# Attention's TensorE instructions in written order, values two steps behind their scores, queries prepared in thirds

## The chip, the cores and the metric

One core of one Trainium2 chip runs the whole program, a two-layer network, in one launch. The metric is the device time of an execution in microseconds (us); lower is better. The engines are TensorE (PE in the profile; PEld is its weight loads), VectorE (DVE), ScalarE (ACT), GpSimd (POOL) and the queue of SyncE (SP), which issues the loads.

## The reference, cut to what matters

Layer 0 is attention over 256 latent and 256 context tokens with 16 heads of 64 and 4 key/value heads. Each latent query sees rotated keys of its window and unrotated context keys; a context query sees context keys alone; a sink logit joins each softmax.

```python
s_win = jnp.einsum('blgrd,bsgd->bgrls', qb, kw) * scale      # rotated q, k; masked to the window
s_ctx = jnp.einsum('blgrd,bsgd->bgrls', qpb, k_c) * scale    # plain q, context k
p = sink_softmax(jnp.concatenate([s_win, s_ctx], axis=-1))
o = einsum(p[..., :SPAN], vw) + einsum(p[..., SPAN:], v_c)
y_lat = o.reshape(...) @ w_out                               # then layer norm, MLP, layer 1 (SSM), MLP
```

## The kernel before

All is float32. A large product is split in a high and a low part (`wh`, `wl`; `u0h`, `u0l`), three matmuls for each tile of 128 (`gemm`, lines 79 to 81). Attention runs over eight pairs of heads, p = 0 to 7, and in each over three items t: t = 0 and 1 are the two blocks of latent queries, t = 2 is both blocks of context queries. Item (p, t) is

- `scores`: ten matmuls (eight for t = 2) into two PSUM banks `s`; DVE takes the maxima (`TENSOR_REDUCE`, lines 461 and 467) and three small operations; ACT does the exponentials into `P` (line 477); DVE two small operations and the division (line 484);
- `mix`: eight transposes `pt` of `P` on PE (line 497), two ACT copies to `PT`, eight (t = 2: four) value matmuls `o` (line 503; each is two rows of the profile), an ACT copy and a DVE subtraction into `oh`, `ol`.

`q_gemm(p)` makes the queries of a pair: 24 matmuls `q` of 512 columns, copied by ACT to `qf`; `q_parts(p)` splits and rotates them on ACT and DVE into `qe, qo, re, ro`, which the scores of pair p read. `filler` is a generator of 27 steps on the modulation vectors: 24 groups of four matmuls `mod<-wm` (line 93), each on its own 512 KB load `wm` with two buffers, and three outputs of two transposes each. The PSUM tags are `mm` (4 banks: scores, most of the query products), `aux` (3: transposes, values) and `md` (1).

Nothing fixes PE's order: every engine executes its own list in order, and a scheduler makes the lists when the program is built, by its own estimate of what is ready. In the code an item's `mix` follows the next item's `scores`; the lists that come out cut one operation's matmuls into another's. Whatever follows attention (the output projection `ao`, and loads that need attention's buffers) starts as attention ends.

Of the kernel before, what the change touches and what calls it, by code (L numbers as in the profile page):

```python
# [8 lines left out]
F32 = mybir.dt.float32  # L9
F32R = mybir.dt.float32r  # L10
# [29 lines left out]
class Net:  # L40
# [23 lines left out]
    def next_w(self, ahead=2, whole=False):  # L64
# [7 lines left out]
            return wh, wl  # L72
        return wh.rearrange("p (k c) -> p k c", c=128), wl.rearrange("p (k c) -> p k c", c=128)

    def gemm(self, ps, w, ah, al, c0, c1, ks=range(8)):
        mm = self.nc.tensor.matmul
        wh, wl = w
        for k in ks:
            mm(ps, wh[:, k, :], ah[k][:, c0:c1], start=(k == 0), stop=False)  # L79
            mm(ps, wh[:, k, :], al[k][:, c0:c1], start=False, stop=False)  # L80
            mm(ps, wl[:, k, :], ah[k][:, c0:c1], start=False, stop=(k == 7))  # L81
# [8 lines left out]
    def mods_mm(self, ps, k, wm):  # L90
        n = wm.shape[1] // 4
        for j in range(4):
            self.nc.tensor.matmul(ps[32 * j:32 * j + 32, 0:n], self.cs[:, k, :], wm[:, j * n:(j + 1) * n],
                                  start=(k == 0), stop=(k == 7))

    def mods_out(self, i, ps, n, cuts, streams=(0, 1)):

        nc = self.nc
        m4 = self.tmp.tile([128, 256], F32, tag="t1", name="m4")[:, :n]
        nc.scalar.copy(m4, ps[:, 0:n])  # L100
        q = n // 128
        pt = ps[:, 256:512]
        for c in range(q):
            nc.tensor.transpose(pt[:, c * 128:(c + 1) * 128], m4[:, c * 128:(c + 1) * 128], self.ident)
        ptv = pt[:, :n].rearrange("p (c j r) -> p j c r", c=q, j=4)
        for j0, w, t in cuts:
            bm = self.vec("bmod")[:, i * 48 + t:i * 48 + t + w]
            for v in streams:
                nc.vector.tensor_tensor(self.mT[i][:, v, t:t + w].rearrange("p (j c) -> p j c", c=q),
                                        ptv[:, j0:j0 + w // q, :, v], bm.rearrange("p (j c) -> p j c", c=q),  # L110
                                        op=ALU.add)
            if 8 <= t < 16 or t == 32:
                m = self.mT[i][:, streams[0]:streams[-1] + 1, t:t + w]
                nc.vector.tensor_scalar(m, m, 1.0, None, op0=ALU.add)
# [44 lines left out]
        yield  # L159

    def run(self, gen):
        for _ in gen:
            pass


    def affine(self, name, gv, bv, streams, scale, shift):
# [271 lines left out]

    def scores(self, p, t, q):
        nc = self.nc  # L440
        mm = nc.tensor.matmul
        qe, qo, re, ro = q
        g = p // 2
        P = [self.ap.tile([128, 512], F32, tag="P", name=f"P{p}{t}{a}", bufs=4) for a in range(2)]
        T = 1 if t < 2 else 2
        mx = self.ap.tile([128, 2, 8], F32, tag="st", name=f"st{p}{t}")
        bs = []
        for a in range(2):
            ps = self.bank("mm", f"s{p}{t}{a}")
            bs.append(ps)  # L450
            plain, rot = (qe, re) if a == 0 else (qo, ro)
            if t < 2:
# [4 lines left out]
                   start=False, stop=True)  # L457
# [24 lines left out]
        for a in range(2):  # L482
            for tt in range(T):
                nc.vector.tensor_scalar(P[a][:, tt * w:tt * w + w], P[a][:, tt * w:tt * w + w],
                                        sm[:, a, tt:tt + 1], None, op0=ALU.mult)
        return P

    def mix(self, p, t, P):
        nc = self.nc
        g = p // 2  # L490
        PT = [self.ap.tile([128, 512], F32, tag="PT", name=f"PT{p}{t}{a}", bufs=3) for a in range(2)]
        for a in range(2):
            pt = self.bank("aux", f"pt{p}{t}{a}")
            for c in range(4):

                o = c if t < 2 else 2 * (c % 2) + c // 2
                nc.tensor.transpose(pt[:, o * 128:o * 128 + 128], P[a][:, c * 128:c * 128 + 128], self.ident)
            nc.scalar.copy(PT[a], pt)
        n, keys = (128, range(4)) if t < 2 else (256, range(2, 4))
        po = self.bank("aux", f"o{p}{t}")[:, :n]  # L500
        for i, kt in enumerate(keys):
            for a in range(2):
                nc.tensor.matmul(po[64 * a:64 * a + 64, :], self.V[:, kt, g * 64:g * 64 + 64],  # L503
                                 PT[a][:, i * n:i * n + n], start=(i == 0), stop=(i == len(keys) - 1))
        c = slice(t * 128, t * 128 + n)
        nc.scalar.copy(self.oh[p][:, c], po)
        nc.vector.tensor_sub(self.ol[p][:, c], po, self.oh[p][:, c].bitcast(F32))
# [23 lines left out]
    def kv_start(self, uh, ul):  # L531
        nc = self.nc
        quarter = self.quarters
        ws = []
        next(quarter)
        ws += [self.next_w(ahead=0) for _ in range(2)]
        next(quarter)
        ws += [self.next_w(ahead=0) for _ in range(2)]

        vs = [(self.oh[q], self.ol[q]) for q in range(4, 8)]  # L540
        for n in range(2):
            self.emit_w(self.wpos, vs[2 * n:2 * n + 2])
            self.wpos += 1
            self.wout += 1
        next(quarter)
        vb = [self.bank("aux", f"v{t}") for t in range(2)]
        k0, q0, k1, q1 = bs = [self.bank(("aux", "mm")[t > 0], f"kq{t}") for t in range(4)]
        nc.vector.tensor_scalar(self.sink8, self.vec("sink"), 8.0, None, op0=ALU.mult)
        self.qs = {}
        for h in range(4):  # L550
            if h < 3:
                next(quarter)
            if h < 2:
                next(quarter)
            for t in range(4):
                self.gemm(bs[t], ws[2 * (t % 2) + t // 2], uh, ul, 0, 512, range(2 * h, 2 * h + 2))
                if h == 3 and t == 0:
                    kr = self.k_rope(k0)
                    self.k_parts(0, k0, kr)
                if h == 3 and t == 1:  # L560
                    self.qs[0] = self.q_parts(0, q0)
            self.v_gemm(vb, vs, uh, ul, range(2 * h, 2 * h + 2))
        for i in range(2):
            nc.scalar.copy(self.V[:, 2 * i:2 * i + 2, :], vb[i].rearrange("p (t d) -> p t d", t=2))
        return k0, kr, k1, q1
# [9 lines left out]
        self.kdup(self.krh, self.krl, g, kr[c, :])  # L575

    def attention(self, uh, ul, filler, k0, kr, k1, q1):
        qs = self.qs
        pend = []
        for p in range(8):  # L580
            q = qs.pop(p)
            for t in range(3):
                P = self.scores(p, t, q)
                pend.append((p, t, P))
                if p == 0 and t == 0:
                    qf = self.q_gemm(2, uh, ul, "aux")
                    self.k_parts(1, k0, kr)
                    kr = self.k_rope(k1)
                    qs[1] = self.q_parts(1, q1)
                if p == 0 and t == 1:  # L590
                    self.k_parts(2, k1, kr)
                    self.k_parts(3, k1, kr)
                for _ in range(1 + (t == 1)):
                    next(filler, None)
                if len(pend) > 1:
                    self.mix(*pend.pop(0))
                if t == 0 and p < 6:
                    qs[p + 2] = self.q_parts(p + 2, qf)
                if t == 1 and p < 5:
                    qf = self.q_gemm(p + 3, uh, ul, "mm")  # L600
        while pend:
            self.mix(*pend.pop(0))

    def q_gemm(self, p, uh, ul, tag):
        w = self.next_w()
        ps = self.bank(tag, f"q{p}")
        self.gemm(ps, w, uh, ul, 0, 512)
        qf = self.ap.tile([128, 512], F32, tag="qf", name=f"qf{p}", bufs=1)
        self.nc.scalar.copy(qf, ps)
        return qf  # L610

    def q_parts(self, p, ps):
        qe = self.aq.tile([128, 512], F32R, tag="qe", name=f"qe{p}", bufs=3)
        qo = self.aq.tile([128, 512], F32R, tag="qo", name=f"qo{p}", bufs=3)
        re = self.aq.tile([128, 256], F32R, tag="re", name=f"re{p}", bufs=3)
        ro = self.aq.tile([128, 256], F32R, tag="ro", name=f"ro{p}", bufs=3)
        self.qsplit(qe, qo, ps)
        qr = self.aq.tile([128, 256], F32, tag="kr", name=f"qr{p}")
        self.rope(qr, ps[:, 0:256])
        self.qsplit(re, ro, qr)  # L620
        return qe, qo, re, ro


    def setup(self, ctx):
        tc, nc, a = self.tc, self.nc, self.a
        self.ctx = ctx
        pool = lambda n, b, **k: ctx.enter_context(tc.tile_pool(name=n, bufs=b, **k))
        self.cst = pool("cst", 1)
        self.xp = pool("xp", 1)
# [537 lines left out]
```

## Time and profile before

| | us |
|---|---|
| median of 3 runs | 1210.81 (1210.56 to 1215.44) |
| the profiled execution | 1204.13 |
| its span in the trace | 1202.3 |
| attention in it: from the first `q` matmul to the end of the last `o` | 63.05 to 217.9 |

The profile is one execution; it lies 6.7 us under the median of the runs. Its times count from the span's start. A matmul's row is longer than its turn on the array, since matmuls are pipelined: a turn is read from one start to the next.

### The profile page before, as it was taken

How to read it: one execution, taken by the hardware profiler on the slowest of the kernel's cores; microseconds unless marked ns; L12 is line 12 of the kernel's file. 1: busy time of each engine (PE TensorE's matmuls, PEld its weight loads, DVE VectorE, ACT ScalarE, POOL GpSimd, SP SyncE). 2: the span in 40 equal slices, each digit the busy share in tenths (PEclk: the TensorE clock that was granted, in tenths of full speed). 3: DMA queues.
4: the chain of work that ended last, by engine and by line, in shares of the span. 5: the costliest groups of instructions: out<-in, count | busy, mean ns of one | idle time of the engine just before them, and what ended most of it. 6: DMA issues, size and time to landing. Idle time of an engine off the chain costs nothing.

```text
span 1202.3 us, 18548 instructions
## 1 busy us (share of the span) xinstructions
PE 1139.5 (95%) x6976; PEld 916.9 (76%) x6976; DVE 845.2 (70%) x1701; ACT 600.7 (50%) x1372; POOL 62.7 (5%) x85
## 2 busy tenths in 40 slices
PE   5999999998999999989999898999999985999996
PEld 4766767887988878868898786777777674898995
DVE  4498677668958677744434889989898678565666
ACT  4376666235512322312323747787968654454551
POOL 1200000005000000000000500000000021000000
PEclk8999999999999999999999999999999997999999
DMA  8735331441645567633222125434544561555551
GB/s 327 296 109 172 110 125 48 136 145 38 206 144 179 167 215 277 222 131 105 93 82 72 44 108 160 141 116 166 171 144 143 215 220 47 188 185 180 197 186 70
DMA packets 41433, 182.79 MB, mean 152 GB/s; under 512 B 4608, under 2 KB 5248, under 8 KB 28288
## 3 DMA queue, kind: packets, MB, share of 16 engines
q1 hardware_dynamic: 41056, 181.36, 44.5%
q8 instruction: 55, 0.90, 0.3%
q10 hardware_dynamic: 288, 0.26, 0.1%
q14 instruction: 34, 0.28, 0.1%
HBM read 180.41 MB, written 1.18 MB: 151 GB/s over the span
## 4 chain that ended last, share of the span: by engine, by line
PE 77%; DVE 11%; DMA 5%; ACT 5%; issue 2%; DVEq 0%; SPq 0%; ACTq 0%
PE f0b L79 5%; PE f0b L81 5%; PE f0b L80 5%; PE f0a L79 5%; PE f0a L80 4%; PE f0a L81 4%; PE y L942 3%; PE o L503 2%; PE f L263 2%; PE f L262 2%; PE f1a L79 2%; PE f1a L81 2%; PE f1a L80 2%; PE f L261 2%; DMA wm<-in_w_mod 2%
## 5 line engine op out<-in xcount | busy, mean ns | idle before, releaser
L61 ACT CAST wh<-raw 128x512 fp32r<-128x512 f32 x404 | 237.4, 619 | 406.5 <-PE f0b L80 126.4
L62 DVE TENSOR_TENSOR wl<-raw,wh 128x512 fp32r<-128x512 f32 x404 | 268.9, 687 | 124.7 <-ACT wh L61 124.0
L80 PE MATMUL f0b<-f0fl,wh 128*128 128x512 f32 (+1 forms) x320 | 111.9, 350 | 3.5 <-DVE f0fl L358 3.5
L79 PE MATMUL f0b<-f0fh,wh 128*128 128x512 f32 (+1 forms) x320 | 114.6, 359 | 0.0
L79 PE MATMUL f0a<-u1h,wh 128*128 128x512 f32 (+1 forms) x320 | 111.4, 350 | 1.5 <-ACT u1h L181 1.5
L81 PE MATMUL f0b<-f0fh,wl 128*128 128x512 f32 (+1 forms) x320 | 112.3, 351 | 0.0
L81 PE MATMUL f0a<-u1h,wl 128*128 128x512 f32 (+1 forms) x320 | 110.9, 347 | 0.0
L80 PE MATMUL f0a<-u1l,wh 128*128 128x512 f32 (+1 forms) x320 | 110.9, 349 | 0.0
L142 DVE SCALAR_TENSOR_TENSOR ma<-wm,cs,ma 128x1024 f32<-128x1024 f32 x70 | 88.7, 1281 | 25.9 <-DMA wm<-in_w_mod 25.7
L80 PEld LDWEIGHTS f0b<-f0fl,wh 128*128 128x128 f32 x320 | 60.5, 189 | 13.6 <-DVE f0fl L358 4.2
L79 PEld LDWEIGHTS f0a<-u1h,wh 128*128 128x128 f32 x320 | 60.3, 189 | 11.7 <-ACT u1h L181 2.3
L81 PEld LDWEIGHTS f0b<-f0fh,wl 128*128 128x128 f32 x320 | 60.6, 189 | 10.5 <-issue 2.1
L79 PEld LDWEIGHTS f0b<-f0fh,wh 128*128 128x128 f32 x320 | 60.4, 189 | 10.6 <-issue 2.6
L81 PEld LDWEIGHTS f0a<-u1h,wl 128*128 128x128 f32 x320 | 60.6, 189 | 8.1 <-issue 0.4
L80 PEld LDWEIGHTS f0a<-u1l,wh 128*128 128x128 f32 x320 | 60.3, 189 | 7.8 <-issue 0.4
L79 PE MATMUL f1a<-u4h,wh 128*128 128x256 f32 x224 | 64.3, 287 | 0.0
L81 PE MATMUL f1a<-u4h,wl 128*128 128x256 f32 x224 | 64.1, 286 | 0.0
L80 PE MATMUL f1a<-u4l,wh 128*128 128x256 f32 x224 | 64.1, 286 | 0.0
L346 DVE SCALAR_TENSOR_TENSOR X<-f0b,mT,X 128x256 f32<-128x256 f32 x48 | 21.0, 479 | 47.2 <-PE f0b L81 47.2
L79 PE MATMUL x<-u2h,wh 128*128 128x512 f32 x128 | 51.3, 401 | 2.1 <-DVE cy L753 2.1
L926 ACT ACTIVATE W<-A,sT 128x128 f32<-128x128 f32 (+1 forms) x128 | 50.0, 458 | 3.8 <-PE y L942 2.5
L81 PE MATMUL x<-u2h,wl 128*128 128x512 f32 x128 | 51.0, 400 | 0.7 <-DVE wl L62 0.7
(438 smaller groups left out, 2760.1 us busy)
## 6 DMA issues: line engine op xcount, KB each, us to landing
raw<-in_wall SPq DMA_DIRECT2D x102, 1024.0 KB, 5.0
wm<-in_w_mod SPq DMA_DIRECT2D x96, 512.0 KB, 4.5
A<-dq SPq DMA_DIRECT2D x32, 256.0 KB, 4.7
E<-dq SPq DMA_DIRECT2D x32, 256.0 KB, 4.9
X<-in_xT SPq DMA_DIRECT2D x8, 256.0 KB, 8.4
gate<-in_rows SPq DMA_DIRECT2D x2, 512.0 KB, 12.3
out_dram<-Xt SPq DMA_DIRECT2D x4, 256.0 KB, 2.0
mixg<-in_rows SPq DMA_DIRECT2D x1, 512.0 KB, 6.1
```

What stands on the lines that cost most here:

```text
L61: nc.scalar.copy(h, src[:, c])
L62: nc.vector.tensor_sub(l, src[:, c], h.bitcast(F32))
L79: mm(ps, wh[:, k, :], ah[k][:, c0:c1], start=(k == 0), stop=False)
L80: mm(ps, wh[:, k, :], al[k][:, c0:c1], start=False, stop=False)
L81: mm(ps, wl[:, k, :], ah[k][:, c0:c1], start=False, stop=(k == 7))
L142: nc.vector.scalar_tensor_tensor(t, wm, c, t, op0=ALU.mult, op1=ALU.add)
L261: mm(ps, lh(i), wh[:, c], start=(k == 0), stop=False)
L262: mm(ps, ll(i), wh[:, c], start=False, stop=False)
L263: mm(ps, lh(i), wl[:, c], start=False, stop=last)
L503: nc.tensor.matmul(po[64 * a:64 * a + 64, :], self.V[:, kt, g * 64:g * 64 + 64], PT[a][:, i * n:i * n + n], start=(i == 0), stop=(i == len ...
L926: nc.scalar.activation(W[:, h, o:o + l1 - l0], A[:, h, l0:l1], AF.Relu, scale=-1.0, bias=self.sT[:, st, r + h:r + h + 1])
L942: mm(ps[64 * a:64 * a + 64, l0:l1], lh[:, hc:hc + 64], mv, start=(n == 0), stop=(n == 5))
```

## The change

Attention's matmuls and transposes are pinned to the order in which the code writes them (`pin`), and the code is rewritten: `mix` is cut into `turn` (transposes, copies) and `mix` (values); in the step of item i come the transposes of item i-2, the scores of item i, at most a third of a query product, one `filler` step (two from p = 6; before one, and two at t = 1), and the values of item i-2. The products of q2 and q3 stay whole: q2 ahead of the first scores, q3 behind them; those of q4 to q7 are cut in 3, 3 and 2 tiles of the contraction (9, 9 and 6 matmuls) at t = 1, 2 and the next 0. `q_parts` is a generator of three parts, one a step. Buffers: `P` 6 for 4, `PT` 4 for 3, `qf` 2 for 1, `qe, qo, re, ro` 2 for 3. No arithmetic is added or removed.

```diff
+    def pin(self, on):
+        if on:
+            self.mm = lambda *a, **k: self.tc.keep_in_program_order(self.nc.tensor.matmul(*a, **k))
+            self.tr = lambda *a, **k: self.tc.keep_in_program_order(self.nc.tensor.transpose(*a, **k))
+        else:
+            self.mm, self.tr = self.nc.tensor.matmul, self.nc.tensor.transpose
...
     def attention(self, uh, ul, filler, k0, kr, k1, q1):
...
+        late, parts = [], []
+        self.pin(True)
+        qg = self.q_gemm(2, uh, ul, "mm", 1)
+        self.run(qg)
         for p in range(8):
+            for _ in self.chain(*parts):
+                pass
             q = qs.pop(p)
             for t in range(3):
-                P = self.scores(p, t, q)
-                pend.append((p, t, P))
+                old = late.pop(0) if len(late) > 1 else None
+                if old is not None:
+                    PT = self.turn(*old)
+                late.append((p, t, self.scores(p, t, q)))
                 if p == 0 and t == 0:
-                    qf = self.q_gemm(2, uh, ul, "aux")
-                    self.k_parts(1, k0, kr)
-                    kr = self.k_rope(k1)
-                    qs[1] = self.q_parts(1, q1)
+                    self.run(self.q_parts(1, q1))
+                    self.run(self.q_gemm(3, uh, ul, "aux", 1))
...
-                for _ in range(1 + (t == 1)):
+                for g in parts:
+                    next(g, None)
+                if t == 1 and 0 < p < 5:
+                    qg = self.q_gemm(p + 3, uh, ul, "mm", 3)
+                next(qg, None)
+                for _ in range(1 if p < 6 else 2):
                     next(filler, None)
-                if len(pend) > 1:
-                    self.mix(*pend.pop(0))
-                if t == 0 and p < 6:
-                    qs[p + 2] = self.q_parts(p + 2, qf)
-                if t == 1 and p < 5:
-                    qf = self.q_gemm(p + 3, uh, ul, "mm")
+                if old is not None:
+                    self.mix(*old[:2], PT)
+            parts = []
+            if p < 6:
+                parts = [self.q_parts(p + 2, self.qfs.pop(p + 2))]
```

The lists show it. First PE's list of before behind the scores of item (4, 1): `pt320` and `pt321` are the two halves of the transposes of item (3, 2), `o32` its values, `q7` the product of pair 7's queries.

```order
L104 MATMUL mod03_1353<-con_78,m4_1814 128x128 x2
L497 MATMUL pt320_1750<-con_78,P320_1655 128x128 x2
L79 MATMUL q7_1858<-u0h0_101,wh11_1391 128x512
L497 MATMUL pt320_1750<-con_78,P320_1655 128x128 x2
L497 MATMUL pt321_1756<-con_78,P321_1656 128x128 x4
L80 MATMUL q7_1858<-u0l0_109,wh11_1391 128x512
L503 MATMUL o32_1762<-PT320_1748,V_144 64x256
L81 MATMUL q7_1858<-u0h0_101,wl11_1392 128x512
L503 MATMUL o32_1762<-PT321_1749,V_144 64x256
L503 MATMUL o32_1762<-PT320_1748,V_144 64x256
```

Transposes, values and the query product alternate. PE's list of the change ahead of the scores of the same item (4, 1) (`s410`), with the last matmul of a third of the product of pair 6's queries (`q6`) at its head:

```order
L78 MATMUL q6_1548<-u0h7_108,wl10_1094 128x512
L78 MATMUL mod03_1481<-wm033_1707,cs_81 32x256 x4
L78 MATMUL o31_1713<-PT310_1658,V_144 64x128
L78 MATMUL o31_1713<-PT311_1659,V_144 64x128
...
L78 MATMUL o31_1713<-PT310_1658,V_144 64x128
L78 MATMUL o31_1713<-PT311_1659,V_144 64x128
L79 MATMUL pt320_1726<-con_78,P320_1585 128x128 x4
L79 MATMUL pt321_1732<-con_78,P321_1586 128x128 x4
L78 MATMUL s410_1741<-krh_140,re4_1416 128x256
L78 MATMUL s410_1741<-krl_141,re4_1416 128x256
```

Each kind now stands in one piece, and the transposes of (3, 2) stand ahead of the scores of (4, 1) instead of behind them. From the first `q` to the last `o`, PE's list changes its kind of matmul 177 times before and 115 times now.

Second, the start of attention on PE, where the product of pair 2's queries (`q2`) and the first scores (`s000`) meet, before:

```order
L80 MATMUL q2_766<-u0l2_111,wh6_746 128x512
L81 MATMUL q2_766<-u0h2_103,wl6_747 128x512
L79 MATMUL q2_766<-u0h3_104,wh6_746 128x512
L454 MATMUL s000_720<-krh_140,re0_659 128x256
L455 MATMUL s000_720<-krl_141,re0_659 128x256
L456 LDWEIGHTS identb_98
```

and now:

```order
L78 MATMUL q2_739<-u0h7_108,wh6_719 128x512
L78 MATMUL q2_739<-u0l7_116,wh6_719 128x512
L78 MATMUL q2_739<-u0h7_108,wl6_720 128x512
L78 MATMUL s000_769<-krh_140,re0_659 128x256
L78 MATMUL s000_769<-krl_141,re0_659 128x256
L78 LDWEIGHTS identb_98
```

The first scores stood behind 10 matmuls of q2 and now stand behind all 24.

Third, PE's list now in pair 6, from the last of the scores of (6, 0) (`s601`) to the first of (6, 1) (`s610`); `wm040` and `wm041` are two loads:

```order
L78 MATMUL s601_2103<-kpl_143,qo6_1864 128x256
L78 MATMUL mod04_2120<-wm040_2121,cs_81 32x256 x4
L78 MATMUL mod04_2120<-wm041_2127,cs_81 32x256 x4
L78 MATMUL o51_2133<-PT510_2079,V_144 64x128
L78 MATMUL o51_2133<-PT511_2080,V_144 64x128
...
L78 MATMUL o51_2133<-PT511_2080,V_144 64x128
L79 MATMUL pt520_2146<-con_78,P520_2015 128x128 x4
L79 MATMUL pt521_2152<-con_78,P521_2016 128x128 x4
L78 MATMUL s610_2161<-krh_140,re6_1865 128x256
```

Two `mod` groups in a row, each on a load of its own, stand ahead of the values of (5, 1) and of the transposes of (5, 2); before, one stood at each step of pair 6.

## Rows read from the trace of the kernel before

**Rows 1.** Chain that ended last, by engine, from the page of the profile.

```profile
PE 77%; DVE 11%; DMA 5%; ACT 5%; issue 2%; DVEq 0%; SPq 0%; ACTq 0%
```

**Rows 2.** Stretches: us; busy PE, PEld, DVE, ACT, POOL; clock, DMA share, GB/s.

```profile
63.05:87.02 23.97, 21.95 (x143) 15.64 (x143) 22.62 (x60) 17.60 (x43) 0.00 (x0) 1.00 0.38 117
87.02:108.50 21.48, 20.03 (x149) 14.03 (x148) 18.27 (x52) 13.51 (x38) 0.00 (x0) 1.00 0.55 189
108.50:128.50 20.00, 19.94 (x145) 14.00 (x144) 13.94 (x46) 12.86 (x36) 0.00 (x0) 1.00 0.27 80
128.50:149.30 20.80, 20.74 (x151) 14.16 (x150) 13.90 (x44) 12.56 (x36) 0.00 (x0) 1.00 0.46 152
149.30:169.55 20.25, 19.47 (x145) 13.87 (x144) 14.06 (x46) 12.95 (x37) 0.00 (x0) 1.00 0.27 78
169.55:183.95 14.40, 14.05 (x119) 8.93 (x117) 12.34 (x43) 9.91 (x32) 0.00 (x0) 1.00 0.66 220
183.95:195.75 11.80, 11.71 (x102) 8.59 (x98) 8.43 (x30) 8.52 (x29) 0.00 (x0) 1.00 0.16 47
195.75:206.70 10.95, 10.72 (x84) 7.80 (x82) 7.81 (x29) 6.59 (x22) 1.01 (x6) 1.00 0.00 1
206.70:217.90 11.20, 10.79 (x90) 8.29 (x88) 5.47 (x21) 7.04 (x23) 0.00 (x0) 1.00 0.01 1
sum 154.85, PE 149.41 PEld 105.31 DVE 116.85 ACT 101.52 POOL 1.01; mean PE 16.60 PEld 11.70 DVE 12.98 ACT 11.28 POOL 0.11
```

**Rows 3.** PE's waits in attention: us in total, times, longest.

```profile
PE pt L497 <- DVE P L484: 2.5, 3, 1.0
...
PE o L503 <- ACT PT L498: 0.6, 2, 0.3
```

**Rows 4.** Timeline of PE: start, us, what; items (3, 2), (4, 0), (4, 1).

```profile
146.86 0.28 PE L465 MATMUL s<-kph,qe 128*128 128x256 f32 x1
...
147.91 0.64 PE L93 MATMUL mod<-wm,cs 128*32 128x256 f32 x8
148.47 1.09 PE L497 MATMUL pt<-con,P 128*128 128x128 f32 x8
149.32 0.36 PE L454 MATMUL s<-krh,re 128*128 128x256 f32 x1
...
151.19 1.09 PE L503 MATMUL o<-PT,V 128*64 128x128 f32 x14
152.21 0.38 PE L460 MATMUL s<-kpl,qo 128*128 128x256 f32 x1
152.52 0.64 PE L93 MATMUL mod<-wm,cs 128*32 128x256 f32 x8
153.09 0.38 PE L454 MATMUL s<-krh,re 128*128 128x256 f32 x1
...
154.39 0.38 PE L104 MATMUL mod<-con,m 128*128 128x128 f32 x2
...
159.36 0.39 PE L80 MATMUL q<-u0l,wh 128*128 128x512 f32 x1
159.59 0.40 PE L81 MATMUL q<-u0h,wl 128*128 128x512 f32 x1
```

**Rows 5.** Timeline of DVE: divisions of (4, 0), (4, 1), (7, 2).

```profile
158.43 0.88 DVE L484 TENSOR_SCALAR P<-P,st 128x512 f32<-128x512 f32 x2
...
164.15 0.88 DVE L484 TENSOR_SCALAR P<-P,st 128x512 f32<-128x512 f32 x2
...
212.44 1.14 DVE L484 TENSOR_SCALAR P<-P,st 128x256 f32<-128x256 f32 x4
```

**Rows 6.** Loads of `wm` in attention, from issue to landing.

```profile
DMA to landing us min/median/max: 3.5/3.7/7.0
```

**Rows 7.** Timeline of PE in layer 0's MLP: a wait, in brackets.

```profile
520.39 0.50 PE L80 MATMUL f0b<-f0fl,wh 128*128 128x512 f32 x1 [3.46 <-DVE f0fl L358]
```

**Rows 8.** A stretch behind that wait; columns as in rows 2.

```profile
522.00:525.00 3.00, 3.00 (x9) 2.32 (x8) 2.12 (x4) 0.06 (x1) 0.00 (x0) 0.50 0.77 254
```

More of the change, by code (lines that the diff above doesn't have):

```diff
@@ L73, in next_w @@
         return wh.rearrange("p (k c) -> p k c", c=128), wl.rearrange("p (k c) -> p k c", c=128)
+    def pin(self, on):
[4 more added lines that the diff above has]
+            self.mm, self.tr = self.nc.tensor.matmul, self.nc.tensor.transpose
     def gemm(self, ps, w, ah, al, c0, c1, ks=range(8)):
-        mm = self.nc.tensor.matmul
+        mm = self.mm
         wh, wl = w
@@ L92, in mods_mm @@
         for j in range(4):
-            self.nc.tensor.matmul(ps[32 * j:32 * j + 32, 0:n], self.cs[:, k, :], wm[:, j * n:(j + 1) * n],
-                                  start=(k == 0), stop=(k == 7))
+            self.mm(ps[32 * j:32 * j + 32, 0:n], self.cs[:, k, :], wm[:, j * n:(j + 1) * n],
+                    start=(k == 0), stop=(k == 7))
     def mods_out(self, i, ps, n, cuts, streams=(0, 1)):
@@ L103, in mods_out @@
         for c in range(q):
-            nc.tensor.transpose(pt[:, c * 128:(c + 1) * 128], m4[:, c * 128:(c + 1) * 128], self.ident)
+            self.tr(pt[:, c * 128:(c + 1) * 128], m4[:, c * 128:(c + 1) * 128], self.ident)
         ptv = pt[:, :n].rearrange("p (c j r) -> p j c r", c=q, j=4)
@@ L161, in run @@
     def run(self, gen):
-        for _ in gen:
+        last = None
+        for last in gen:
             pass
+        return last
     def affine(self, name, gv, bv, streams, scale, shift):
@@ L440, in scores @@
         nc = self.nc
-        mm = nc.tensor.matmul
+        mm = self.mm
         qe, qo, re, ro = q
         g = p // 2
-        P = [self.ap.tile([128, 512], F32, tag="P", name=f"P{p}{t}{a}", bufs=4) for a in range(2)]
+        P = [self.ap.tile([128, 512], F32, tag="P", name=f"P{p}{t}{a}", bufs=6) for a in range(2)]
         T = 1 if t < 2 else 2
@@ L486, in scores, with turn @@
         return P
-    def mix(self, p, t, P):
+    def turn(self, p, t, P):
         nc = self.nc
-        g = p // 2
-        PT = [self.ap.tile([128, 512], F32, tag="PT", name=f"PT{p}{t}{a}", bufs=3) for a in range(2)]
+        PT = [self.ap.tile([128, 512], F32, tag="PT", name=f"PT{p}{t}{a}", bufs=4) for a in range(2)]
         for a in range(2):
@@ L496, in mix @@
                 o = c if t < 2 else 2 * (c % 2) + c // 2
-                nc.tensor.transpose(pt[:, o * 128:o * 128 + 128], P[a][:, c * 128:c * 128 + 128], self.ident)
+                self.tr(pt[:, o * 128:o * 128 + 128], P[a][:, c * 128:c * 128 + 128], self.ident)
             nc.scalar.copy(PT[a], pt)
+        return PT
+    def mix(self, p, t, PT):
+        nc = self.nc
+        g = p // 2
         n, keys = (128, range(4)) if t < 2 else (256, range(2, 4))
@@ L502, in mix @@
             for a in range(2):
-                nc.tensor.matmul(po[64 * a:64 * a + 64, :], self.V[:, kt, g * 64:g * 64 + 64],
-                                 PT[a][:, i * n:i * n + n], start=(i == 0), stop=(i == len(keys) - 1))
+                self.mm(po[64 * a:64 * a + 64, :], self.V[:, kt, g * 64:g * 64 + 64],
+                        PT[a][:, i * n:i * n + n], start=(i == 0), stop=(i == len(keys) - 1))
         c = slice(t * 128, t * 128 + n)
@@ L548, in kv_start @@
         nc.vector.tensor_scalar(self.sink8, self.vec("sink"), 8.0, None, op0=ALU.mult)
-        self.qs = {}
+        self.qs, self.qfs = {}, {}
         for h in range(4):
@@ L560, in kv_start @@
                 if h == 3 and t == 1:
-                    self.qs[0] = self.q_parts(0, q0)
+                    self.run(self.q_parts(0, q0))
             self.v_gemm(vb, vs, uh, ul, range(2 * h, 2 * h + 2))
@@ L578, in attention @@
         qs = self.qs
-        pend = []
+        late, parts = [], []
+        self.pin(True)
+        qg = self.q_gemm(2, uh, ul, "mm", 1)
+        self.run(qg)
         for p in range(8):
+            for _ in self.chain(*parts):
+                pass
             q = qs.pop(p)
             for t in range(3):
-                P = self.scores(p, t, q)
-                pend.append((p, t, P))
+                old = late.pop(0) if len(late) > 1 else None
+                if old is not None:
+                    PT = self.turn(*old)
+                late.append((p, t, self.scores(p, t, q)))
@@ L585, in attention @@
                 if p == 0 and t == 0:
-                    qf = self.q_gemm(2, uh, ul, "aux")
+                    self.run(self.q_parts(1, q1))
+                    self.run(self.q_gemm(3, uh, ul, "aux", 1))
+                if p == 0 and t == 1:
                     self.k_parts(1, k0, kr)
                     kr = self.k_rope(k1)
-                    qs[1] = self.q_parts(1, q1)
-                if p == 0 and t == 1:
                     self.k_parts(2, k1, kr)
                     self.k_parts(3, k1, kr)
-                for _ in range(1 + (t == 1)):
-                    next(filler, None)
@@ L595, in attention @@
-                if len(pend) > 1:
-                    self.mix(*pend.pop(0))
-                if t == 0 and p < 6:
-                    qs[p + 2] = self.q_parts(p + 2, qf)
-                if t == 1 and p < 5:
-                    qf = self.q_gemm(p + 3, uh, ul, "mm")
-        while pend:
-            self.mix(*pend.pop(0))
-    def q_gemm(self, p, uh, ul, tag):
+                for g in parts:
+                    next(g, None)
+                if t == 1 and 0 < p < 5:
+                    qg = self.q_gemm(p + 3, uh, ul, "mm", 3)
@@ L605, in q_gemm @@
+                next(qg, None)
+                for _ in range(1 if p < 6 else 2):
+                    next(filler, None)
+                if old is not None:
[3 more added lines that the diff above has]
+                parts = [self.q_parts(p + 2, self.qfs.pop(p + 2))]
+        for old in late:
+            self.mix(*old[:2], self.turn(*old))
+        self.pin(False)
+    def q_gemm(self, p, uh, ul, tag, parts):
         w = self.next_w()
         ps = self.bank(tag, f"q{p}")
-        self.gemm(ps, w, uh, ul, 0, 512)
@@ L608, in q_gemm @@
-        qf = self.ap.tile([128, 512], F32, tag="qf", name=f"qf{p}", bufs=1)
-        self.nc.scalar.copy(qf, ps)
-        return qf
-    def q_parts(self, p, ps):
[L613 to L616, printed above, removed]
+        cut = [0, 8] if parts == 1 else [0, 3, 6, 8]
@@ new lines, in q_gemm @@
+        for n in range(parts):
+            self.gemm(ps, w, uh, ul, 0, 512, range(cut[n], cut[n + 1]))
+            if n == parts - 1:
+                qf = self.qfs[p] = self.ap.tile([128, 512], F32, tag="qf", name=f"qf{p}")
+                self.nc.scalar.copy(qf, ps)
+            yield self.qfs.get(p)
+    def q_parts(self, p, ps):
+        qe = self.aq.tile([128, 512], F32R, tag="qe", name=f"qe{p}", bufs=2)
+        qo = self.aq.tile([128, 512], F32R, tag="qo", name=f"qo{p}", bufs=2)
+        re = self.aq.tile([128, 256], F32R, tag="re", name=f"re{p}", bufs=2)
+        ro = self.aq.tile([128, 256], F32R, tag="ro", name=f"ro{p}", bufs=2)
+        self.qs[p] = (qe, qo, re, ro)
@@ L617, in q_parts @@
         self.qsplit(qe, qo, ps)
+        yield
         qr = self.aq.tile([128, 256], F32, tag="kr", name=f"qr{p}")
         self.rope(qr, ps[:, 0:256])
+        yield
         self.qsplit(re, ro, qr)
-        return qe, qo, re, ro
+        yield
     def setup(self, ctx):
@@ L626, in setup @@
         self.ctx = ctx
+        self.pin(False)
         pool = lambda n, b, **k: ctx.enter_context(tc.tile_pool(name=n, bufs=b, **k))
```

## Prediction

> **What bounds the kernel now.** I read the chain that ended last first: PE holds 77% of it, DVE 11%, loads 5% [rows 1]. So time goes where PE's own list is long or waits. What follows attention has the same lists in both kernels and starts as attention ends, so only 63.05 to 217.9 counts, and a microsecond there is one of the whole. I cut it into nine stages, at the first scores of pairs 1 to 7, the end of the last scores and of the last values, and read each engine's busy time in them [rows 2]. The reader is to see that in the third to fifth stage (a pair of heads each; 20.00, 20.80, 20.25 us) PE is busy nearly throughout and DVE for 13.9 to 14.1 us; that DVE is busy 22.62 of 23.97 us in the first stage and 18.27 of 21.48 in the second; and that the clock is 1.00, the higher level, in all nine. Of PE's waits, those for a divided `P` are 2.5 us in three [rows 3]: PE hardly waits.
>
> A busy PE is not at its peak, so I read turns, from start to start, in its timeline [rows 4]: a query matmul 0.23 (159.36 to 159.59); scores of a latent item in one piece 1.30 (153.09 to 154.39), of a context item 1.05 (146.86 to 147.91); a `mod` group 0.56 and 0.57; eight transposes 0.85 (148.47 to 149.32); values 1.02 for 14 rows (151.19 to 152.21), so 1.17 for 16, and with 0.2 for coming to them from another kind 1.37. Scores and values cut into each other took 3.20 (149.32 to 152.52), where the two apart are 2.67: mixing cost 0.53 for two or three more switches, some 0.2 each.
>
> **The change part by part.** *One kind at a time, stages three to five.* A pair is now three steps in written order:
> step 0: 0.85 + 1.30 + six query matmuls 1.38 + `mod` 0.57 + 1.37 = 5.47;
> step 1: the same with nine, 2.07: 6.16;
> step 2: 0.85 + 1.05 + 2.07 + 0.57 + 1.37 = 5.91.
> Together 17.54, with 0.2 for small waits and outputs of `mod` 17.75, so 53.3 for three pairs where 61.05 stood: **-7.8**. In it is one `mod` group a pair less (1.7 in all), which comes back below. As a check, 62 changes of kind fewer at 0.2 are 12 us over all of attention. What covers the chain from scores to `P` here: from the end of an item's scores to its transposes PE has the rest of that step and the whole next one, 9.6 to 10 us.
>
> The chain itself I read for (4, 0) and (4, 1): scores end at 152.52 and 154.39 [rows 4], divisions at 158.43 + 0.88 and 164.15 + 0.88 [rows 5], so 6.8 and 10.6 us; the second stood behind the parts of a query preparation on DVE, which now come in thirds. I take 8 to 8.7, between the ends: under 9.6, so no wait in these stages.
>
> *First stage, 23.97.* The first scores stand behind 14 more matmuls of q2, 3.2 us later. PE's list is not the limit, DVE's 22.62 of work is, and that starts on key preparation without the scores. I take 22.7, **-1.3**; were DVE idle for those 3.2 us, it would be +1.9.
>
> *Second stage, 21.48.* PE's list is 4.09 + 6.16 + 5.91 = 16.2. Two steps here lack a query product, so PE has only 6.05 (0.57 + 1.37, then a step of 4.09) between an item's scores and its transposes; against 8.7 that is a wait of 2.6, behind which scores, `mod` and values stand on PE, and DVE waits for those scores. 18.8, just above DVE's 18.27: **-2.7**.
>
> *Sixth, 14.40.* 5.47 + 4.09 + 3.84 = 13.4, and a wait of 1.9 (8 less 6.05) for `P` of (5, 1), in a stage in which DVE is busy 12.34: 15.3, **+0.9**.
>
> *Seventh, 11.80.* Two `mod` groups a step: three steps of 0.85 + 1.30 (1.05) + 1.13 + 1.37 = 13.7. Each group needs a load, of 3.5, 3.7 or at most 7.0 us to landing [rows 6]; two buffers serve two groups a step, so the second of a pair is issued when the first of its pair is through. I put 1.0 on the stage for such waits (0, if all land in a step's 4.6 us; 3.3, if one is as late as the latest): 14.7, **+2.9**. Behind a waiting `mod` stand the values, then the next transposes.
>
> *Eighth, 10.95.* 4.65 + 3.8 + 1.9 = 10.4: **-0.5**.
>
> *Tail, 11.20.* The last scores ended at 206.7 and the last division at 212.44 + 1.14, 6.9 us later, with the division of (7, 1) and its small steps, 1.4, ahead of it on DVE [rows 5]. Those now have a step's lead, so 5.5; then 0.85 + 0.3 (the copy's wait [rows 3]) + 1.37: 8.0 to, with nothing gained in the chain, 9.4. I take 8.3, **-2.9**.
>
> *At nothing:* deeper `P`, `PT` and `qf` take waits away that cost PE nothing before; `qe` to `ro` with two buffers are written when the scores of two pairs before are through, one step earlier on PE; the loads of weights, earlier on SP, stand ahead of `mod` loads, and would cost at most the 3.3 already taken, where their buffer is late.
>
> The sum is -1.3 - 2.7 - 7.8 + 0.9 + 2.9 - 0.5 - 2.9 = **-11.4**. To it comes **+1.5** for the clock. The longest wait before was 1.0 us in attention, at clock 1.00 [rows 2, 3]; in layer 0's MLP a wait of 3.46 us [rows 7] was followed by 3.00 us at 0.50, the lower level [rows 8], half of which is lost: 1.5. My longest wait is 2.6, between the two, and I count one fall. -9.9: the profiled execution goes from 1204.1 to 1194.2. The runs' median lies 6.7 us above that execution, so I subtract from the median: **1201**, attention ending at about 208.
>
> The Trainium skill speaks against the waits (TensorE: Matmul & The Clock Gate, "HAM oscillation — how this bites in real kernels"): TensorE that idles for its input between short bursts is throttled again at each such gap. Rows 7 and 8 agree for one gap; the shorter waits of rows 3 cost no clock. By the rule, if each of three waits of about 2 us counted, the sum would be -6.9, by the rows' 1.0 us end -11.4.
>
> **The rivals.** *Only the waits of PE can be saved, as it is busy anyway.* PE is busy 149.41 of 154.85 us [rows 2]; 5.4 us less at most. Against it speak the turns: a row of 14 values counts 1.09 us as busy and gives way after 1.02, and mixing cost 0.53 that counts as busy [rows 4]. With waits of 4.5 at thin places and the gap closed it nets to about -1 to -5, 1208. The Trainium skill, too, says that a matmul's busy share is a poor measure of TensorE's headroom, as pipelined matmuls look other than they cost (Perfetto Trace Analysis, "Identifying the Most-Contended Engine"); the mixed piece agrees.
>
> *DVE takes the gain.* DVE executes in order, and with the lists so pinned a late preparation holds the next maxima. If the pairs stay at 20 us for that, -7.8 goes, and -2.1 is left: 1208 to 1209. For it: 14 of 17.75 us is a fuller DVE than 14 of 20.35. Against: it is still a fifth idle.
>
> *Slower: the transposes in front.* PE now stands still for `P` of item i-2 with the scores of item i behind it, so in the 11 steps without a query product (second, sixth, seventh, eighth stage) the chain sets the step: two steps are the chain plus 2.15 (0.85 + 1.30), so a chain of 10.6 makes a step 6.4 instead of 4.1, 25 us over 11 steps, of which 4.5 is in my sum: +20.5 on -9.9, about 1221. It decides above 9 us (11 steps longer by 1.45, 16 us, less the 4.5). For it: 10.6 was seen. Against: that was behind a preparation, of which pairs 6 and 7 have none, and 6.8 stands beside it.
>
> *More gain:* PE's list alone, with no wait of those (2.6 + 1.9 + 1.0) and no fall of clock: -9.9 - 7.0, 1194.
>
> **How the numbers follow.** My forecast 0.50, more gain 0.12, the two that leave a few microseconds 0.22 together, the transposes in front 0.16. A difference under 0.5%, 6 us, is about what a measurement of this kernel cannot tell from none. So faster 0.62, same 0.22, slower 0.16. The range reaches from 1191, below the gain of the bare list, to 1213, past the cases with little gain; it leaves out the slower case. The forecast's own is 1196 to 1205 (the bounds of the first stage, loads and tail: 3.2, 2.3, 1.1).
>
> **What would show it.** Right: the first scores of pairs 2 to 5 about 17.8 us apart, last values at about 208, each kind of matmul in one run, waits for `P` in the second and sixth stage of 2 to 3 us. Wrong: pairs still 20 us apart with waits for `P` (DVE), steps of 6 us in pairs 6 and 7, waits for `wm` over 1 us a step, a first stage longer than before, or a clock of 0.50 over more than a few microseconds.

## The result and the profile after

The change runs in 1195.47 us (median of 4, 1194.45 to 1197.81), before in 1210.85 (median of 4): the ratio is 0.9867, interval 0.9839 to 0.9895, 15.4 us of medians where 9.9 were forecast. The profiled execution has a span of 1193.4 us, 8.9 less than that of before; the first experiment tells where the other 6.5 are.

Attention by the same nine stages as in [rows 2], now with the bounds of the changed kernel (us; busy PE, PEld, DVE, ACT, POOL; clock, DMA share, GB/s):

```profile
62.85:86.40 23.55, 21.21 (x135) 16.57 (x133) 22.54 (x58) 17.55 (x42) 0.00 (x0) 0.93 0.48 157
86.40:104.53 18.13, 15.77 (x137) 11.62 (x136) 17.57 (x56) 12.17 (x37) 0.00 (x0) 1.00 0.42 123
104.53:120.88 16.35, 16.35 (x137) 12.75 (x136) 14.53 (x45) 13.03 (x41) 0.00 (x0) 1.00 0.29 92
120.88:137.50 16.62, 16.62 (x144) 12.59 (x142) 13.64 (x43) 11.88 (x36) 0.00 (x0) 1.00 0.46 136
137.50:154.11 16.61, 16.61 (x143) 12.57 (x142) 13.59 (x43) 12.13 (x36) 0.00 (x0) 1.00 0.32 96
154.11:168.48 14.37, 12.40 (x120) 9.64 (x118) 12.43 (x45) 12.18 (x40) 0.00 (x0) 0.99 0.50 175
168.48:185.53 17.05, 14.32 (x142) 10.07 (x141) 11.22 (x37) 10.67 (x32) 0.00 (x0) 0.91 0.52 162
185.53:194.90 9.37, 8.92 (x89) 6.82 (x87) 6.55 (x24) 5.46 (x15) 0.55 (x4) 1.00 0.12 45
194.90:204.38 9.48, 9.42 (x81) 7.19 (x79) 4.38 (x17) 5.87 (x20) 0.46 (x3) 1.00 0.00 0
sum 141.53, PE 131.63 PEld 99.81 DVE 116.44 ACT 100.94 POOL 1.01; mean PE 14.63 PEld 11.09 DVE 12.94 ACT 11.22 POOL 0.11
```

141.53 in place of 154.85: 13.3 less. In the third to fifth stage PE was busy for 60.15 of 61.05 us before and is busy for all of 49.58 now. Some of the 11.5 us is moved work: three filler steps went from these pairs to pairs 6 and 7, and with the filler's old rhythm (below) the three stages take 51.5. The other 9.6 us were lost by the same matmuls, nearly all of it time that the busy column had counted as work. The waits of PE in attention, to be set beside [rows 3] (us in total, times, longest):

```profile
PE pt L79 <- DVE P L494: 3.8, 2, 2.0
PE mod L78 <- DMA wm<-in_w_mod: 3.2, 4, 1.9
PE s L78 <- ACT P L487: 1.7, 1, 1.7
```

PE now idles 9.9 us of attention where it idled 5.4 before, and is faster for all that. The step of item (4, 1) in PE's timeline, where each kind stands in one piece, answers to [rows 4]:

```profile
141.82 1.09 PE L79 MATMUL pt<-con,P 128*128 128x128 f32 x8
142.66 0.36 PE L78 MATMUL s<-krh,re 128*128 128x256 f32 x1
...
143.94 0.39 PE L78 MATMUL q<-u0h,wh 128*128 128x512 f32 x1
...
145.75 0.39 PE L78 MATMUL q<-u0h,wl 128*128 128x512 f32 x1
146.07 0.64 PE L78 MATMUL mod<-wm,cs 128*32 128x256 f32 x8
146.64 1.08 PE L78 MATMUL o<-PT,V 128*64 128x256 f32 x8
147.65 1.09 PE L79 MATMUL pt<-con,P 128*128 128x128 f32 x8
148.50 0.36 PE L78 MATMUL s<-kph,qe 128*128 128x256 f32 x1
```

From start to start: transposes 0.84, scores 1.28, nine query matmuls 2.13, `mod` 0.57, values 1.01, together 5.83 us where I had 6.16. And the losses: a wait for a PSUM bank in the first stage and one for `P` in the second, a wait for `P` at the end of the sixth, behind it the clock, and loads in the seventh (the bracket is the wait):

```profile
81.72 0.39 PE L78 MATMUL s<-kph,qo 128*128 128x256 f32 x1 [1.75 <-ACT P L487]
...
91.27 0.92 PE L79 MATMUL pt<-con,P 128*128 128x128 f32 x5 [1.83 <-DVE P L494]
...
167.45 1.37 PE L79 MATMUL pt<-con,P 128*128 128x128 f32 x8 [1.97 <-DVE P L494]
168.48 0.56 PE L78 MATMUL s<-krh,re 128*128 128x256 f32 x1
...
170.94 1.35 PE L78 MATMUL mod<-wm,cs 128*32 128x256 f32 x16
...
175.73 0.64 PE L78 MATMUL mod<-wm,cs 128*32 128x256 f32 x8 [0.20 <-DMA wm<-in_w_mod]
176.96 0.64 PE L78 MATMUL mod<-wm,cs 128*32 128x256 f32 x8 [0.59 <-DMA wm<-in_w_mod]
...
183.09 0.64 PE L78 MATMUL mod<-wm,cs 128*32 128x256 f32 x8 [1.95 <-DMA wm<-in_w_mod]
```

The scores behind the wait of 1.97 took 168.48 to 170.94, 2.46 us for 1.28. Two stretches of attention stand at the lower level of the clock:

```profile
83.00:86.00 3.00, 3.00 (x25) 2.63 (x22) 2.87 (x8) 2.30 (x7) 0.00 (x0) 0.50 0.56 161
168.50:171.50 3.00, 3.00 (x20) 2.36 (x22) 2.84 (x10) 2.35 (x5) 0.00 (x0) 0.50 0.00 0
```

### The profile page after: what moved, and what is told of

The parts are those of the page before. It is cut to its first block, busy times and chain, and to the rows that moved or that the text cites. A ratio compares the mean times of both kernels' runs of the same rounds, so it can differ in the third digit from the quotient of the medians.

```text
span 1193.4 us, 18550 instructions
## 1 busy us (share of the span) xinstructions
PE 1124.8 (94%) x6976; PEld 913.6 (77%) x6976; DVE 844.6 (71%) x1701; ACT 599.7 (50%) x1372; POOL 61.4 (5%) x85
## 4 chain that ended last, share of the span: by engine, by line
PE 74%; DVE 10%; DMA 8%; ACT 5%; issue 2%; DVEq 0%; SPq 0%; ACTq 0%
DMA wm<-in_w_mod 5%; PE f0b L89 5%; PE f0b L87 5%; PE f0b L88 5%; PE f0a L87 4%; PE f0a L88 4%; PE f0a L89 4%; PE y L978 3%; PE f L273 2%; PE f L272 2%; PE f1a L87 2%; PE f1a L89 2%; PE f1a L88 2%; PE f L271 2%; PE q L78 2%
```

## The experiments

In what follows "stages three to five" are pairs 2 to 4 (before 61.05, the change 49.58), and "attention" is its length in the profiled execution (before 154.85, the change 141.53).

**The kernel before once more.** No edit.

> The kernel before once more, to see each run's span and clock. Theory A: the profiled execution shown for it, 1204.13, lay under its runs because a stretch at clock 0.50 that the others have was missing in it; then the new profile or the spans come out near 1208 to 1213 with at least one more such stretch (1.5 to 2 us each) or a longer wait of PE. Theory B: the runs and the profile differ by something ahead of or behind the span; then the spans are again 1202 and the times 1210.

Measured: 1209.64 (1203.9 to 1213.61, 10 runs), the profiled one 1210.26 with a span of 1208.5. Theory A. Against the earlier profile of the same program attention took 1.6 us longer and what follows it 4.7 (989.1 for 984.5). Two of its stretches, in windows; in the earlier profile the clock was 1.00 from 93 to 98 and from 290 to 296:

```profile
93.00:98.00 5.00, 4.52 (x18) 3.56 (x18) 4.97 (x21) 2.06 (x6) 0.00 (x0) 0.66 0.52 200
292.00:296.00 4.00, 3.90 (x20) 3.90 (x21) 4.00 (x10) 1.98 (x5) 3.27 (x4) 0.57 0.02 4
```

In attention the two profiles differ by the stretch behind 94 us alone; the other eight stages agree within 0.02 us. PE's waits ahead of it are the same in both too. In the second profile they were these (0.93 and 0.48 in the earlier one, which stayed at 1.00):

```profile
91.96 0.38 PE L454 MATMUL s<-krh,re 128*128 128x256 f32 x1 [0.94 <-ACT P L477]
...
94.21 0.68 PE L79 MATMUL q<-u0h,wh 128*128 128x512 f32 x1 [0.48 <-ACT P L477]
```

So the profile that I summed against was a lucky execution; behind attention the change takes 989.1 too, what the second profile of before takes. Nothing of the gain is given back later: 14.9 us in attention between these two profiles, 15.4 between the medians.

**No pin.**

```diff
-        self.pin(True)
+        self.pin(False)
```

> The change with the pin alone taken away, so that the scheduler orders TensorE again. Theory (order is the gain): its list changes kind about 29 times more often than the change's; at 0.2 us each some 6 us are lost, 1200 to 1203, and the pairs stand about 18 to 19 us apart in place of 16.5. Rival (the rewritten code and its buffers are the gain, the pin nothing): within 2 us of the change, 1194 to 1197.

Measured: 1193.09 (1192.76 to 1196.41), ratio to before 0.9870 (0.9837 to 0.9902), the change's own. The theory fell. The third to fifth stage, in one window, and from there to the end of the last scores:

```profile
103.64:154.15 50.51, 50.42 (x409) 38.25 (x408) 42.96 (x136) 37.95 (x112) 0.00 (x0) 1.00 0.36 107
154.15:192.07 37.92, 37.53 (x346) 26.54 (x345) 29.85 (x105) 28.29 (x88) 1.01 (x6) 1.00 0.46 151
```

Two of the three pairs take 16.61 us each, pinned or not: left free, PE's list came out in whole pieces there by itself: of its 29 changes of kind more, counted in the traces, one lies in these stages. At the thin places a free list puts other work in front of what is late: waits for `P` are 0.4 us and for `wm` 0.9 (3.8 and 3.2 pinned), the clock is 1.00 throughout, and the stages from the sixth to the eighth take 37.9 us for 40.8. Attention is 139.6, 1.9 shorter, in a profile without a fall of the clock where that of the change has two. The pin bought nothing; that it cost anything is not shown.

**The filler's old rhythm, pinned.**

```diff
-                for _ in range(1 if p < 6 else 2):
+                for _ in range(1 + (t == 1)):
```

> The change with the old rhythm of the filler: one step, at t = 1 two, so that no pairs of mod groups on two fresh loads stand in pairs 6 and 7. Theory (the 3.2 us of waits for wm there are the doubled steps' cost): seventh stage 13 to 14 us in place of 17.05, pairs 2 to 5 0.6 us longer each, attention 1 to 2.5 us shorter, 1193 to 1195. Rival (the loads come late by SyncE's order whatever the rhythm): waits for wm of 3 us or more elsewhere, attention no shorter, 1195 to 1198.

Measured: 1197.98 (1194.65 to 1201.77), 0.9903 (0.9870 to 0.9936); attention 141.9. The seventh stage fell to 12.8, as the theory had it, but stages three to five rose to 51.5 and the sixth to 15.5, and PE's waits for `wm` became 4.3 us in place of 3.2. The rival holds: in the pinned order two groups in one step wait for loads wherever they stand. Before, with the same rhythm in a free order, PE's list of waits in attention has none for `wm`.

**One step's lag, pinned.**

```diff
-                old = late.pop(0) if len(late) > 1 else None
-                if old is not None:
-                    PT = self.turn(*old)
+                old = late.pop(0) if late else None
...
-                    self.mix(*old[:2], PT)
+                    self.mix(*old[:2], self.turn(*old))
```

> The change with the transposes and the values of item i-1, together, behind the scores, query third and filler step of item i, pinned: one step's lag as before. Theory (the lag of two steps pays): between scores and transposes PE has about 8.4 us in steps with a query third and 4.3 without, and the values follow their copy at once, waiting about 0.6 us 24 times; with the thin steps' waits 15 to 25 us more than the change, 1210 to 1220. Rival (only that each kind stands in one piece pays): 1194 to 1199.

Measured: 1230.45 (1227.51 to 1235.97), 1.0176 (1.0138 to 1.0214); attention 184.3. The theory's direction, but 35 us more than the change where it said 15 to 25. PE's waits:

```profile
PE o L78 <- ACT PT L508: 24.2, 24, 2.1
PE pt L79 <- DVE P L494: 5.5, 3, 2.1
```

All 24 items wait for the copy of their transposes, 1.0 us each where I had 0.6, and the clock stood at 0.50 in six stretches of attention, over 3 us each. Pinned order without the lag is 20 us slower than before.

**One step's lag, free.** Both edits above, of the pin and of the lag.

> The change without the pin and with one step's lag: transposes and values of item i-1 together behind the scores of item i, query products still in thirds. Its TensorE list changes kind about as often as that of before (168 to 171 by one count, where the change without the pin has 137). Theory (the lag of two steps is the gain, because it lets a free order keep one kind together): pairs 2 to 4 take about 20 us again, 1206 to 1212. Rival (the products and their preparation in thirds are the gain): pairs 16.5 to 17 us, 1193 to 1198.

Measured: 1205.17 (1200.77 to 1208.24, 10 runs), 0.9971 (0.9951 to 0.9990); attention 152.3, stages three to five 54.9. The total is near the theory (just under its range), the pairs between theory and rival: the thirds do shorten these, and it is given back in the later stages.

**Whole query products, free, two steps' lag.**

```diff
-                for g in parts:
-                    next(g, None)
+                for g in parts:
+                    self.run(g)
...
-                    qg = self.q_gemm(p + 3, uh, ul, "mm", 3)
+                    qg = self.q_gemm(p + 3, uh, ul, "mm", 1)
```

> The change without the pin, with each query product whole at t = 1 and its preparation in one go, as before; the lag of two steps stays. Theory (the lag is the gain): within 3 us of the change without the pin, 1191 to 1197, pairs 16.5 to 17.2 us. Rival (the thirds keep DVE and PE in step): maxima and divisions held behind a whole preparation on DVE, pairs of 18.5 us or more, 1200 to 1208.

Measured: 1197.16 (1194.93 to 1199.60), 0.9914 (0.9887 to 0.9941); attention 142.2, stages three to five 52.3. The theory, just past its edges: in profiles that both stood at clock 1.00, the thirds are worth 2.6 us of attention beside the lag. The intervals of the two ratios overlap, so the time alone does not show it.

**The lag alone, in the kernel before** (`turn` cut out of `mix` as in the change; `P` 6 for 4).

```diff
+                old = pend.pop(0) if len(pend) > 1 else None
+                if old is not None:
+                    PT = self.turn(*old)
                 P = self.scores(p, t, q)
                 pend.append((p, t, P))
...
-                if len(pend) > 1:
-                    self.mix(*pend.pop(0))
+                if old is not None:
+                    self.mix(*old[:2], PT)
```

> The kernel before with one part of the change alone: transposes cut from the values and both two steps behind the scores (P in 6 buffers for it); no pin, query products whole, their preparation in one go, filler as before. Theory (the lag of two steps is nearly the whole gain): attention 141 to 146 us, pairs 2 to 4 at 17 to 18 us, 1194 to 1201. Rival (it needs the thirds or the deeper qf and PT beside it): pairs above 19 us, 1203 to 1208.

Measured: 1199.35 (1194.44 to 1203.87, 6 runs), 0.9938 (0.9914 to 0.9962); attention 146.1 (with one stretch at 0.50 in its second stage), stages three to five 54.1. The lag alone gives 8.8 of the 13.3 us of attention, and about half of the medians' gain (8.1). The theory named the largest part but called it nearly the whole, which it is not.

**Values woven into the query product, pinned.** Between two value matmuls stands one of the query third of the same step, which so comes behind the filler step; nothing else moves.

```diff
+    def gemm_steps(self, ps, w, ah, al, c0, c1, ks):
...
                         PT[a][:, i * n:i * n + n], start=(i == 0), stop=(i == len(keys) - 1))
+                next(weave, None)
...
-                next(qg, None)
+                third = iter(lambda: next(qg, True), True)
...
-                    self.mix(*old[:2], PT)
+                    self.mix(*old[:2], PT, third)
+                for _ in third:
+                    pass
```

> The change, pinned, with the values of item i-2 woven one by one into the third of the query product in the same step: the same instructions, lag and buffers, 124 more changes of kind. Theory (a change of kind costs PE about 0.2 us): 20 to 28 us more than the change, 1215 to 1224, pairs 2 to 4 about 21 us in place of 16.5. Rival (mixing costs nothing, the longer pairs of before were waits that the view counts as busy): 1194 to 1199.

Measured: 1225.81 (1223.64 to 1226.75), 1.0147 (1.0127 to 1.0167); attention 171.6, 30.0 more than the change, pairs 2 to 4 24.3 to 24.6 us. The theory, a little above its size. The timeline shows the price without any wait between the rows:

```profile
126.38 0.43 PE L78 MATMUL o<-PT,V 128*64 128x128 f32 x2
126.74 0.49 PE L78 MATMUL q<-u0h,wh 128*128 128x512 f32 x1
127.16 0.43 PE L78 MATMUL o<-PT,V 128*64 128x128 f32 x2
127.52 0.49 PE L78 MATMUL q<-u0l,wh 128*128 128x512 f32 x1
```

One value matmul takes 0.36 and one query matmul 0.42, 0.78 for both; in their pieces they take 0.13 (1.03 for eight) and 0.23. Going there and back costs 0.42 us, 0.21 a change. This is the price of going to or from a value. Not every change has one: in the kernel before, a query matmul gave way to transposes after 0.23 us, as to another query, and to values after 0.43:

```profile
157.59 0.49 PE L81 MATMUL q<-u0h,wl 128*128 128x512 f32 x1
158.02 1.08 PE L503 MATMUL o<-PT,V 128*64 128x256 f32 x6
...
159.83 0.40 PE L79 MATMUL q<-u0h,wh 128*128 128x512 f32 x1
160.06 1.04 PE L497 MATMUL pt<-con,P 128*128 128x128 f32 x8
```

To a `mod` group it was 0.32 (145.75 to 146.07 in the change). Counted in the traces, stages three to five of before hold 54 changes to or from a value or a `mod` group and 20 among queries, scores and transposes; the change holds 26 and 19. Between them stand the kernel without the pin with 29, whole products with 33, the lag alone with 34 (and the old filler), and one step's lag, free, with 44; these stages take 50.5, 52.3, 54.1 and 54.9 us in that order.

**The doubled filler early, free, then pinned.**

```diff
-                for _ in range(1 if p < 6 else 2):
+                for _ in range(2 if p < 2 else 1):
```

> The change without the pin, and with the doubled filler steps in pairs 0 and 1, where DVE sets the time, in place of pairs 6 and 7. Theory (PE idles under DVE's work in the first two stages and is full from the third on): six mod groups of 0.57 us move beneath DVE, attention 2.5 to 3.5 us shorter than without the pin alone, 1189 to 1191.5. Rival (the loads for them come late there, or DVE's order gains nothing): 1192.5 to 1197.

> The change, pinned, with the doubled filler steps in pairs 0 and 1 in place of pairs 6 and 7 (pair 6 then has one mod group a step, pair 7 none). Theory A (of the seventh stage's 17.1 us the waits for wm and the doubled groups are the surplus): no wait for wm over 1 us, seventh stage 11.5 to 12.5, attention 136 to 138.5, 1189 to 1192. Theory B (the groups and even the waits lay in time in which PE would have waited for a divided P): waits for P in pairs 6 and 7 rise by 3 us or more, attention 140 to 142, 1193 to 1197.

Measured: free 1193.49 (1192.07 to 1195.47), 0.9883 (0.9862 to 0.9904), attention 138.5, 1.1 less than without the pin alone; what follows attention took 992.3 in its profile, 3.3 more, so the time does not show it: the rival's times. Pinned 1194.49 (1193.05 to 1195.21), 0.9859 (0.9844 to 0.9874), attention 139.5. Theory A was right of the seventh stage (11.75 us), but the loads were waited for in the first, which rose to 26.7; the time is theory B's, though PE's waits for `P` did not rise. The clock was 1.00 throughout attention, in spite of a wait of 2.2 us. PE's waits pinned:

```profile
PE mod L78 <- DMA wm<-in_w_mod: 6.2, 5, 2.2
PE pt L79 <- DVE P L494: 3.7, 3, 1.9
```

**Three steps' lag, pinned, then with the doubled filler early** (`P` 8, `PT` 2).

```diff
-                old = late.pop(0) if len(late) > 1 else None
+                old = late.pop(0) if len(late) > 2 else None
```

> The change, pinned, with transposes and values three steps behind their scores (P in 8 buffers, PT in 2). Theory (what the pinned change still loses are PE's waits for P at the thin steps and the clock that falls behind them): no wait for P over 0.5 us, no stretch at 0.50 in attention, sixth stage 11 to 12 us in place of 14.4, tail at most 1.5 longer, attention 136 to 139, 1189 to 1193. Rival (the waits go over to a PSUM bank or to DVE, which sets these places): attention 140.5 or more, 1194 to 1198.

> Both at once: three steps' lag and the doubled filler steps in pairs 0 and 1, pinned. Theory (the two losses are apart): attention 132.5 to 136, 1185 to 1190. Rival (either takes what the other gives, since DVE fills the first two stages): attention 137 or more, 1191 to 1196.

Measured: 1199.54 (1194.03 to 1206.21, 7 runs), 0.9916 (0.9886 to 0.9947), attention 145.3; with the filler early 1197.30 (1196.62 to 1197.97), 0.9884 (0.9869 to 0.9898), attention 144.0. Both rivals. The waits for `P` are gone and the sixth stage is 12.3 us, as the theory said, but PE waits for a PSUM bank instead (with the filler early, 4.9 us for `wm`), the clock stood at 0.50 for some 10 us of the first two stages in the first of the two, and the tail, with one item more behind the last scores, takes 13.5 for 9.5. PE's waits in the first of the two:

```profile
PE s L78 <- ACT P L487: 2.9, 1, 2.9
PE q L78 <- ACT P L487: 2.5, 1, 2.5
```

No version is told apart from the change as faster: the ratios without the pin, 0.9870, and with the filler early, 0.9883 and 0.9859, stand within its interval.

## Why the prediction was right, by its own steps

The direction and the range held; the gain was half as large again as forecast, so that the time lies just under the forecast's own 1196 to 1205, and one of its reasons was given to the wrong part of the change.

*Stages three to five*, -7.8: measured -11.5. The mechanism is shown (the woven kernel: 0.21 us a change, against the 0.2 taken from [rows 4]), but for changes to or from values and `mod` groups, not for each change of kind, as the check with 62 changes had it. The size failed in one term. I put 0.2 for coming to the values on top of their 1.17, which I had scaled from 14 rows, in every step; in whole pieces the values take 1.01 to 1.03 in all, 0.35 less a step, 3.2 over nine steps, and the 0.2 a pair for small waits was not needed. A piece's turn, read to the start of the next, already holds what its border costs. The account is not closed: 28 such changes fewer at 0.21 are 5.9 of the 9.6 us that the same matmuls lost, and no run prices the other 3.7.

*What keeps a kind together.* I took the pinned order for the cause and the lag for the risk. The free kernel shows pairs of 16.61 us without the pin, and the lag alone in the kernel before gave 8.8 us. Pinned without the lag is 1230. So over all of attention the lag of two steps is the larger cause (8.8 us alone), the thirds and deeper buffers the smaller (2.6 without the lag); in stages three to five the two alone are nearer to each other, 7.0 and 6.2, the latter with the three filler steps fewer. The thirds and the buffers are not told apart, and the pin gained nothing. Why the lists come out so is read from their order only and not shown: with two steps the scheduler's own estimate would have the transposes ready when the code names them.

*First and second stage*, -1.3 and -2.7: measured -0.4 and -3.4, together 41.68 us with DVE busy 40.1. DVE is the floor there, as said; the wait for `P` is 1.83 in place of 2.6, and a wait of 1.75 for a bank, which I had not, came before it.

*Sixth*, +0.9: 0.0, with the forecast wait (1.97 for 1.9) and a shorter list. *Seventh*, +2.9: +5.3. The waits for `wm` are 2.7 in place of 1.0, and the clock's fall lies here, 1.2 us on the scores alone. *Eighth* -0.5: -1.6. *Tail* -2.9: -1.7. My cut at 195.75 was not the first score of pair 7, which the list of before had at 195.29, between scores of pair 6; with it the seventh is +5.7 and the eighth -2.0.

*The clock*, one fall for 1.5: two falls, after waits of 1.75 and 1.97 us; waits of 1.83 (before 91.27) and 1.95 (before 183.09) were followed by none. The rule of the Trainium skill that I weighed (TensorE: Matmul & The Clock Gate, "HAM oscillation — how this bites in real kernels") says that TensorE which waits for its input between short bursts is throttled again at each such wait; the waits of its example are longer than these. The rows agree for two of four waits of this length.

*Subtracting from the median* was right, and for a reason now shown: the profiled execution of before had fewer falls of the clock than the second one, which lies near the runs' median.

*The rivals.* "Only PE's waits can be saved" is refuted: PE's busy time itself fell from 149.41 to 131.63. The page that I named against it (the Trainium skill, Perfetto Trace Analysis, "Identifying the Most-Contended Engine") says that a matmul's busy share is a poor measure of TensorE's headroom. The trace agrees: busy nearly throughout, these stages still gave up 9.6 us. "DVE takes the gain" holds in the first two stages alone. "The transposes in front" did not come: only two of the 11 thin steps waited for `P`, 1.83 and 1.97 us. The steps of pair 6 took 5.6, 5.3 and 6.1 us, near the sign of being wrong that I had named, but stretched by the clock and by loads rather than by `P`. "More gain" (1194) came nearest in time, and not by its condition: the waits and the falls that it left out did come, and the pairs gave more than it had.

Open is what makes the clock fall. It fell after two of the four waits here, not after one of 2.2 us with the filler early, and in the second profile of before behind no wait above 0.94, where the earlier profile had the same waits and no fall. Open is also why the kernel with the shortest attention (138.5) took 3.3 us more behind it in its profile than the one without the pin.

## What to carry to other kernels

A TensorE that is busy all the time may still lose a sixth to changes between kinds of matmul that alternate one by one: price a turn from start to start, in one piece and mixed, before taking the busy column for a bound, and do it for each pair of kinds, as here only the changes to and from values and `mod` groups cost. To keep kinds together, give the consumer more lag (here two steps; a third gained nothing) before writing an order by hand: with the lag the free order came out nearly the same where it mattered, and it bent at the thin places where the pinned one waited. And put a forecast on the runs' median: one profiled execution can lie 6 us off it.

## What the runs showed of the hardware

A change between a value matmul and a query matmul cost 0.21 us (0.78 for the two against 0.36 in pieces); one from a query to transposes cost nothing that the starts show (0.23, as between queries). In the change the granted clock fell to 0.50, the lower level, for 3 to 4 us behind waits of PE of 1.75 and 1.97 us, and not behind waits of 1.83 and 1.95. The length of a wait did not decide it: of two profiles of the kernel before with the same waits of PE, none above 1.0 us in attention, one fell to 0.50 there and the other did not. Executions of this one program spread from 1203.9 to 1213.6 us, and its two profiles, 1204.1 and 1210.3, have mean clocks of 0.984 and 0.980.
